# A batched matmul limited by its transfers: all loads first and all stores after, in place of loads mixed with stores

## The chip, the cores and the metric

The kernel runs on one core of a Trainium2 chip, the other cores idle. The metric is device time in microseconds (us), the median of several executions. A profile is one further execution; its span runs from the first to the last instruction and is about 2 us shorter than the device time.

Names: PE is the matmul engine (TensorE), ACT is ScalarE, DVE is VectorE, POOL is GpSimd, SP is the engine that issues the transfers here. In lines of the profile PEld is PE loading the stationary operand, and a q after an engine's name (SPq) is its sequencer, which issues instructions; PSUM is the memory that PE writes to. The granted clock is the share of PE's full clock that the trace records as let through. A transfer is cut over the core's 16 DMA engines, and the trace has a record of every packet: start, duration, size. A packet here is one contiguous run of one partition: 4 KB for loads, 16 KB for stores (8 KB for eight of them in the kernel before). Means of packet durations below are taken over all packets of a size in the trace. "Landings" are the semaphore updates of a transfer, one from each DMA engine.

## The reference

```python
batch, n_heads, seq_t, seq_s, channels = 8, 12, 512, 512, 64
x: (8, 12, 512, 64) float32        y: (8, 12, 512, 64) float32
out = np.einsum('bhtc,bhsc->bhts', x, y)     # (8, 12, 512, 512) float32
```

There are 96 heads. The inputs are 25.17 MB and the output 100.66 MB, so four fifths of all bytes are stores.

## The kernel before

Heads are taken in 12 groups of 8. A group's x and y are loaded as float32 (two loads of 1 MB), cast to bf16 by POOL, transposed by PE, copied out of PSUM by DVE and ACT, and then used in four results of two heads each (2 MB). Groups are pipelined: loads run three groups ahead, the transposes of group g + 1 are mixed into the results of group g, and each result is stored as soon as it is made.

```python
AHEAD = 3
lpool = tile_pool(bufs=AHEAD)      # loads, float32
bpool = tile_pool(bufs=2)          # bf16
tpool = tile_pool(bufs=2)          # transposed, bf16
opool = tile_pool(bufs=6)          # results, 16 KB per partition
...
def prepare(g, made):              # a generator, five steps
    ...                            # POOL casts x and y of group g to bf16
    if g + AHEAD < NG:
        load(g + AHEAD)
    yield
    ...                            # 16 transposes of y on PE, copies by DVE and ACT; then x
...
for g in range(NG):
    xT, yT = made.pop(g)
    steps = prepare(g + 1, made) if g + 1 < NG else iter(())
    for a in range(2):
        for pair in range(2):
            ot = opool.tile([P, K, S], fp32)
            edge = (g == 0 and a == 0) or (g == NG - 1 and a == 1)
            for k in range(K // 2):
                if (pair * K // 2 + k) in (0, 3, 6):
                    next(steps, None)
                pm = pmpool.tile([P, 2, S], fp32)
                ...                # 4 matmuls of 64x512 into pm
                ...                # ACT (k even) or DVE (k odd) copies pm to ot
                if edge and k % 2 == 1:
                    ...            # the first two and last two results: stored in halves of 1 MB
            if not edge:
                nc.sync.dma_start(ov[g, 2 * a + pair], otf)
```

Of the kernel before, what the change touches and what calls it, by code (L numbers as in the profile page):

```python
# [1 line left out]

# [5 lines left out]


@with_exitstack  # L10
def kernel(
    ctx: ExitStack,
    tc: tile.TileContext,
    x: bass.AP,
    y: bass.AP,
    out: bass.AP,
):





    nc = tc.nc
    B, H, T, C = x.shape
    _, _, S, _ = y.shape
    P = 128
    G = 4
    Q = P // G
    R = T // Q
    NG = B * H // (2 * G)  # L30
    K = R // 2
    AHEAD = 3
    fp32 = mybir.dt.float32
    bf16 = mybir.dt.bfloat16
    COPY = mybir.ActivationFunctionType.Copy
    assert C * 2 == P and S == T and R == 16

    xv = x.rearrange("b h t c -> (b h t c)").rearrange("(g a p n) -> g p a n", a=2, p=P, n=R * C)
    yv = y.rearrange("b h t c -> (b h t c)").rearrange("(g a p n) -> g p a n", a=2, p=P, n=R * C)
    ov = out.rearrange("b h t s -> (b h t s)").rearrange("(g a p n) -> g a p n", a=4, p=P, n=K * S)  # L40

    const = ctx.enter_context(tc.tile_pool(name="const", bufs=1))
    lpool = ctx.enter_context(tc.tile_pool(name="lpool", bufs=AHEAD))
    bpool = ctx.enter_context(tc.tile_pool(name="bpool", bufs=2))
    tpool = ctx.enter_context(tc.tile_pool(name="tpool", bufs=2))
    opool = ctx.enter_context(tc.tile_pool(name="opool", bufs=6))
    ptpool = ctx.enter_context(tc.tile_pool(name="ptpsum", bufs=2, space=bass.MemoryType.PSUM))
    pmpool = ctx.enter_context(tc.tile_pool(name="pmpsum", bufs=3, space=bass.MemoryType.PSUM))

    loaded = {}  # L50

    def load(g):
        xs = lpool.tile([P, 2, R, C], fp32)
        ys = lpool.tile([P, 2, R, C], fp32)
        nc.sync.dma_start(ys.rearrange("p a r c -> p a (r c)"), yv[g])  # L55
        nc.sync.dma_start(xs.rearrange("p a r c -> p a (r c)"), xv[g])  # L56
        loaded[g] = (xs, ys)

    for g in range(AHEAD):
        load(g)  # L60

    ident = const.tile([P, P], bf16)
    make_identity(nc, ident)

    def prepare(g, made):

        xs, ys = loaded.pop(g)
        yb = bpool.tile([P, R, 2, C], bf16)
        xb = bpool.tile([P, R, 2, C], bf16)
        for s, b in ((ys, yb), (xs, xb)):  # L70
            for half in range(2):
                rows = slice(half * K, (half + 1) * K)
                nc.gpsimd.tensor_copy(b[:, rows], s[:, :, rows].rearrange("p a r c -> p r a c"))  # L73
        if g + AHEAD < NG:
            load(g + AHEAD)
        yield
        yT = tpool.tile([P, G * Q, R], bf16)
        xT = tpool.tile([P, K, P, 2], bf16)
        for half in range(2):
            pt = ptpool.tile([P, K, P], bf16)  # L80
            for k in range(K):
                nc.tensor.transpose(  # L82
                    pt[:, k, :], yb[:, half * K + k].rearrange("p a c -> p (a c)"), ident
                )
            dst = yT[:, :, half * K:(half + 1) * K]
            src = pt.rearrange("p k n -> p n k")
            if half == 0:
                nc.vector.tensor_copy(dst, src)  # L88
            else:
                nc.scalar.activation(dst, src, COPY)  # L90
            yield
        for half in range(2):
            pt = ptpool.tile([P, K, P], bf16)
            for k in range(K):
                e, i = divmod(k, K // 2)
                nc.tensor.transpose(  # L96
                    pt[:, k, :], xb[:, e * K + half * K // 2 + i].rearrange("p a c -> p (a c)"), ident
                )
            dst = xT[:, half * K // 2:(half + 1) * K // 2]
            src = pt.rearrange("p (e i) n -> p i n e", e=2)  # L100
            if half == 0:
                nc.vector.tensor_copy(dst, src)  # L102
            else:
                nc.scalar.activation(dst, src, COPY)  # L104
            yield
        made[g] = (xT, yT.rearrange("p n k -> p (n k)"))

    made = {}
    for _ in prepare(0, made):
        pass  # L110
    for g in range(NG):
        xT, yT = made.pop(g)
        steps = prepare(g + 1, made) if g + 1 < NG else iter(())
        for a in range(2):
            for pair in range(2):
                ot = opool.tile([P, K, S], fp32)
                otf = ot.rearrange("p r s -> p (r s)")
                edge = (g == 0 and a == 0) or (g == NG - 1 and a == 1)
                for k in range(K // 2):
                    if (pair * K // 2 + k) in (0, 3, 6):  # L120
                        next(steps, None)
                    pm = pmpool.tile([P, 2, S], fp32)
                    for two in range(2):
                        for h in range(2):
                            col = (2 * pair + h) * Q
                            nc.tensor.matmul(  # L126
                                pm[h * 64:(h + 1) * 64, two, :],
                                xT[a * C:(a + 1) * C, 2 * k + two, col:col + Q].rearrange("c n e -> c (n e)"),
                                yT[a * C:(a + 1) * C, (2 * pair + h) * S:(2 * pair + h + 1) * S],
                                start=True, stop=True,  # L130
                            )
                    if k % 2 == 0:
                        nc.scalar.activation(ot[:, 2 * k:2 * k + 2, :], pm, COPY)  # L133
                    else:
                        nc.vector.tensor_copy(ot[:, 2 * k:2 * k + 2, :], pm)  # L135
                    if edge and k % 2 == 1:
                        i, j = (2 * k - 2) * S, (2 * k + 2) * S
                        nc.sync.dma_start(ov[g, 2 * a + pair][:, i:j], otf[:, i:j])
                if not edge:
                    nc.sync.dma_start(ov[g, 2 * a + pair], otf)  # L140


# [1 line left out]
_INS = ['x', 'y']  # L144
_OUTS = [((8, 12, 512, 512), 'float32')]


# [23 lines left out]
```

## Time and profile before

| | before |
|---|---|
| time, median (3 runs) | 306.62 us (306.41 to 306.93) |
| profiled span | 304.3 us |
| q1 (all loads and stores), share of 16 engines' time | 98.2% |
| PE, DVE, ACT busy | 69%, 48%, 39% |
| mean packet: 4 KB load, 8 KB store, 16 KB store | 163.4, 309.4, 612.3 ns |
| landings of the last store: first, mean, last | 296.6, 298.7, 303.2 us |

From the page of the kernel before: the span; then the span in 40 slices (PE busy and DMA busy in tenths, PE's granted clock in tenths, GB/s moved); then the queue of all loads and stores, and the queue of instruction fetches (count, MB, share of 16 engines).

```profile
span 304.3 us, 2968 instructions
PE   0899999999959538928946844893897797671000
PEclk9999999999999855555555655555555555555555
DMA  7999999999999999999999999999999999999992
GB/s 283 411 410 418 436 429 423 419 442 405 445 419 419 430 431 421 420 437 424 426 426 435 414 429 433 413 433 429 433 433 429 431 433 429 428 428 433 423 420 89
q1 hardware_dynamic: 14016, 125.83, 98.2%
q8 instruction: 9, 0.15, 0.2%
```

DMA stays at 9 from the second slice to the last but one. That is the bound (q1 98.2% of 16 engines' time); PE has gaps (69% busy). The traffic is 410 to 433 GB/s over the longer stretches; single slices between the second and the last but one show 405 to 445.

One caution on the clock row: the trace's first clock record is at 98.0 us here, and the 9s before it have no record behind them. Transposes start 107 ns apart there (median), as in stretches recorded at 0.50.

The table of stretches of the kernel before (start:end, length, busy time of PE, weight load, DVE, ACT, POOL, PE's clock, DMA share, GB/s), first two stages, then the end:

```profile
12.00:20.00 8.00, 7.61 (x42) 3.29 (x43) 4.68 (x5) 4.06 (x4) 6.31 (x7) 1.00 1.03 410
180.00:220.00 40.00, 25.53 (x141) 13.16 (x141) 18.28 (x16) 14.70 (x15) 6.07 (x6) 0.50 1.01 429
...
295.00:300.00 5.00, 0.00 (x0) 0.00 (x0) 0.00 (x0) 0.00 (x0) 0.00 (x0) 0.50 0.57 243
300.00:304.30 4.30, 0.00 (x0) 0.00 (x0) 0.00 (x0) 0.00 (x0) 0.00 (x0) 0.50 0.08 34
```

Loads alone run at 410 GB/s, mixed traffic and stores at 424 to 433 (stretches of 10 us and more). The last two lines show a fade: for six microseconds only some of the 16 DMA engines still work (DMA share 0.57, then 0.08). The 16 landings of the last store come one by one, from 296.6 to 303.2 us. The kernel ends with the slowest engine (the span ends at 304.3 us).

### The profile page before, as it was taken

How to read it: one execution, taken by the hardware profiler on the slowest of the kernel's cores; microseconds unless marked ns; L12 is line 12 of the kernel's file. 1: busy time of each engine (PE TensorE's matmuls, PEld its weight loads, DVE VectorE, ACT ScalarE, POOL GpSimd, SP SyncE). 2: the span in 40 equal slices, each digit the busy share in tenths (PEclk: the TensorE clock that was granted, in tenths of full speed). 3: DMA queues.
4: the chain of work that ended last, by engine and by line, in shares of the span. 5: the costliest groups of instructions: out<-in, count | busy, mean ns of one | idle time of the engine just before them, and what ended most of it. 6: DMA issues, size and time to landing. Idle time of an engine off the chain costs nothing.

```text
span 304.3 us, 2968 instructions
## 1 busy us (share of the span) xinstructions
PE 208.5 (69%) x1152; PEld 104.6 (34%) x1152; DVE 144.7 (48%) x120; ACT 119.4 (39%) x121; POOL 49.3 (16%) x54
## 2 busy tenths in 40 slices
PE   0899999999959538928946844893897797671000
PEld 0444344555425114513613522541453443330000
DVE  0456666567446435616525733743565664443000
ACT  1454645364445224624515512542364552522000
POOL 3773220400500310230050050031000000000000
PEclk9999999999999855555555655555555555555555
DMA  7999999999999999999999999999999999999992
GB/s 283 411 410 418 436 429 423 419 442 405 445 419 419 430 431 421 420 437 424 426 426 435 414 429 433 413 433 429 433 433 429 431 433 429 428 428 433 423 420 89
DMA packets 14031, 126.03 MB, mean 414 GB/s; under 512 B 1216, under 2 KB 1216, under 8 KB 7360
## 3 DMA queue, kind: packets, MB, share of 16 engines
q1 hardware_dynamic: 14016, 125.83, 98.2%
q8 instruction: 9, 0.15, 0.2%
q14 instruction: 6, 0.05, 0.0%
HBM read 25.17 MB, written 100.66 MB: 413 GB/s over the span
## 4 chain that ended last, share of the span: by engine, by line
DMA 60%; PE 23%; DVE 4%; ACT 2%; issue 1%; POOL 1%; SPq 0%; ACTq 0%
DMA out_dram<-ot 48%; PE pm L126 17%; DMA xs<-in_x_dram 12%; PE pt L82 3%; PE pt L96 3%; DVE ot L135 2%; ACT ot L133 2%; DVE xT L102 1%; POOL xb L73 1%; SPq L55 0%; ACTq L133 0%; SPq L140 0%; ACT xT L104 0%; SPq L56 0%
## 5 line engine op out<-in xcount | busy, mean ns | idle before, releaser
L126 PE MATMUL pm<-yT,xT 64*64 64x512 bf16 x768 | 164.0, 610 | 56.0 <-ACT ot L133 53.9
L135 DVE COPY ot<-pm 128x1024 f32<-128x1024 f32 x96 | 117.2, 1223 | 113.3 <-PE pm L126 57.3
L133 ACT ACTIVATE ot<-pm 128x1024 f32<-128x1024 f32 x96 | 95.1, 1023 | 113.7 <-DMA out_dram<-ot 81.2
L126 PEld LDWEIGHTS <-xT 64*64 64x64 bf16 x768 | 66.1, 150 | 131.2 <-issue 122.7
L73 POOL CAST yb<-ys 128x1024 bf16<-128x1024 f32 x24 | 24.3, 1040 | 140.5 <-DMA ys<-in_y_dram 94.7
L82 PE MATMUL pt<-ident,yb 128*128 128x128 bf16 x192 | 23.7, 307 | 10.7 <-POOL yb L73 6.9
L73 POOL CAST xb<-xs 128x1024 bf16<-128x1024 f32 x24 | 24.3, 1040 | 16.3 <-issue 6.9
L82 PEld LDWEIGHTS <-yb 128*128 128x128 bf16 x192 | 19.9, 143 | 20.3 <-issue 11.5
L96 PE MATMUL pt<-ident,xb 128*128 128x128 bf16 x192 | 24.9, 310 | 1.1 <-POOL xb L73 0.9
L96 PEld LDWEIGHTS <-xb 128*128 128x128 bf16 x192 | 19.1, 141 | 19.3 <-issue 17.8
L104 ACT ACTIVATE xT<-pt 128x1024 bf16<-128x1024 bf16 x12 | 12.3, 1024 | 32.9 <-PE pt L96 29.4
L102 DVE COPY xT<-pt 128x1024 bf16<-128x1024 bf16 x12 | 14.7, 1223 | 10.8 <-PE pt L96 9.4
L88 DVE COPY yT<-pt 128x1024 bf16<-128x1024 bf16 x12 | 14.6, 1216 | 8.9 <-PE pt L82 8.9
L90 ACT ACTIVATE yT<-pt 128x1024 bf16<-128x1024 bf16 x12 | 12.3, 1022 | 9.3 <-PE pt L82 7.7
L90 ACT ACT_TABLE_LOAD x1 | 1.3, 1283 | 0.7 <-PEq L155 0.7
masks.py:199 POOL TENSOR_SCALAR_AFFINE_SELECT ident<-ident 128x128 bf16<-128x128 bf16 x1 | 0.3, 292 | 0.1
masks.py:197 POOL MEMSET ident<- 128x128 bf16 x1 | 0.2, 204 | 0.3 <-POOLq L155 0.3
L155 POOL MEMSET const-float32-0.0<- 128x1 f32 x1 | 0.1, 98 | 0.2 <-issue 0.2
L155 POOL MEMSET const-bfloat16-1.0<- 128x1 bf16 x1 | 0.1, 101 | 0.0
L155 POOL MEMSET const-uint8-127<- 128x1 uint8 x1 | 0.1, 101 | 0.0
L155 POOL MEMSET const-float32-1.0<- 128x1 f32 x1 | 0.1, 98 | 0.0
## 6 DMA issues: line engine op xcount, KB each, us to landing
out_dram<-ot SPq DMA_DIRECT2D x44, 2048.0 KB, 28.3
ys<-in_y_dram SPq DMA_DIRECT2D x12, 1024.0 KB, 20.3
xs<-in_x_dram SPq DMA_DIRECT2D x12, 1024.0 KB, 22.2
out_dram<-ot SPq DMA_DIRECT2D x8, 1024.0 KB, 21.0
```

The source lines that it names most:

```text
L73: nc.gpsimd.tensor_copy(b[:, rows], s[:, :, rows].rearrange("p a r c -> p r a c"))
L82: nc.tensor.transpose(pt[:, k, :], yb[:, half * K + k].rearrange("p a c -> p (a c)"), ident)
L88: nc.vector.tensor_copy(dst, src)
L90: nc.scalar.activation(dst, src, COPY)
L96: nc.tensor.transpose(pt[:, k, :], xb[:, e * K + half * K // 2 + i].rearrange("p a c -> p (a c)"), ident)
L102: nc.vector.tensor_copy(dst, src)
L104: nc.scalar.activation(dst, src, COPY)
L126: nc.tensor.matmul(pm[h * 64:(h + 1) * 64, two, :], xT[a * C:(a + 1) * C, 2 * k + two, col:col + Q].rearrange("c n e -> c (n e)"), yT[a * ...
L133: nc.scalar.activation(ot[:, 2 * k:2 * k + 2, :], pm, COPY)
L135: nc.vector.tensor_copy(ot[:, 2 * k:2 * k + 2, :], pm)
L155: nc = _bacc.Bacc("TRN2", target_bir_lowering=False, num_devices=1)
```

## The change

The intent: never mix reads and writes of memory, by loading everything first. The transposed x and y of all groups stay on chip as bf16: 12 groups x 8 KB, 96 KB of each partition. The six 16 KB buffers that received loads then become the six buffers of the results. All 48 stores are whole tiles of 2 MB.

```diff
-    AHEAD = 3
+    NB = 6
-    lpool = ...(bufs=AHEAD)   bpool (bufs=2)   tpool (bufs=2)   opool (bufs=6)
+    dpool = ctx.enter_context(tc.tile_pool(name="dpool", bufs=NB))
+    bpool = ctx.enter_context(tc.tile_pool(name="bpool", bufs=3))
+    xpool = ctx.enter_context(tc.tile_pool(name="xpool", bufs=NG))
+    ypool = ctx.enter_context(tc.tile_pool(name="ypool", bufs=NG))
...
-                edge = (g == 0 and a == 0) or (g == NG - 1 and a == 1)
-                    if edge and k % 2 == 1:
-                        i, j = (2 * k - 2) * S, (2 * k + 2) * S
-                        nc.sync.dma_start(ov[g, 2 * a + pair][:, i:j], otf[:, i:j])
-                if not edge:
-                    nc.sync.dma_start(ov[g, 2 * a + pair], otf)
+    def result(o, steps):
+        ot = buffer()                       # from dpool, as the loads
+        for k in range(K // 2):
+            next(steps, None)
+            ...                             # matmuls and copies as before
+        nc.sync.dma_start(ov[o], ot)
+    for g in range(NB + 1):
+        for _ in prepare(g):
+            pass
+    for o in range(G * NG):
+        g = NB + 1 + o
+        result(o, prepare(g) if g < NG else iter(()))
```

More of the change, by code (lines that the diff above doesn't have):

```diff
@@ L35, with buffer @@
     COPY = mybir.ActivationFunctionType.Copy
-    assert C * 2 == P and S == T and R == 16
+    assert C * 2 == P and S == T and R == 16 and 4 * R * C == K * S
     xv = x.rearrange("b h t c -> (b h t c)").rearrange("(g a p n) -> g p a n", a=2, p=P, n=R * C)
     yv = y.rearrange("b h t c -> (b h t c)").rearrange("(g a p n) -> g p a n", a=2, p=P, n=R * C)
-    ov = out.rearrange("b h t s -> (b h t s)").rearrange("(g a p n) -> g a p n", a=4, p=P, n=K * S)
+    ov = out.rearrange("b h t s -> (b h t s)").rearrange("(o p n) -> o p n", p=P, n=K * S)
     const = ctx.enter_context(tc.tile_pool(name="const", bufs=1))
-    lpool = ctx.enter_context(tc.tile_pool(name="lpool", bufs=AHEAD))
-    bpool = ctx.enter_context(tc.tile_pool(name="bpool", bufs=2))
-    tpool = ctx.enter_context(tc.tile_pool(name="tpool", bufs=2))
-    opool = ctx.enter_context(tc.tile_pool(name="opool", bufs=6))
+    dpool = ctx.enter_context(tc.tile_pool(name="dpool", bufs=NB))
+    bpool = ctx.enter_context(tc.tile_pool(name="bpool", bufs=3))
+    xpool = ctx.enter_context(tc.tile_pool(name="xpool", bufs=NG))
+    ypool = ctx.enter_context(tc.tile_pool(name="ypool", bufs=NG))
     ptpool = ctx.enter_context(tc.tile_pool(name="ptpsum", bufs=2, space=bass.MemoryType.PSUM))
     pmpool = ctx.enter_context(tc.tile_pool(name="pmpsum", bufs=3, space=bass.MemoryType.PSUM))
+    def buffer():
+        data = dpool.tile([P, K * S], fp32)
+        return data
     loaded = {}
     def load(g):
-        xs = lpool.tile([P, 2, R, C], fp32)
-        ys = lpool.tile([P, 2, R, C], fp32)
-        nc.sync.dma_start(ys.rearrange("p a r c -> p a (r c)"), yv[g])
-        nc.sync.dma_start(xs.rearrange("p a r c -> p a (r c)"), xv[g])
-        loaded[g] = (xs, ys)
-    for g in range(AHEAD):
+        data = buffer()
+        n = 2 * R * C
+        for i, v in enumerate((yv, xv)):
+            nc.sync.dma_start(data[:, i * n:(i + 1) * n].rearrange("p (a n) -> p a n", a=2), v[g])
+        loaded[g] = [data[:, i * n:(i + 1) * n].rearrange("p (a r c) -> p a r c", a=2, r=R) for i in range(2)]
+    for g in range(NB):
         load(g)
@@ L63, with prepare @@
     make_identity(nc, ident)
-    def prepare(g, made):
-        xs, ys = loaded.pop(g)
-        yb = bpool.tile([P, R, 2, C], bf16)
-        xb = bpool.tile([P, R, 2, C], bf16)
-        for s, b in ((ys, yb), (xs, xb)):
+    made = {}
+    def prepare(g):
+        halves = []
+        for s in loaded.pop(g):
+            b = bpool.tile([P, R, 2, C], bf16)
             for half in range(2):
@@ L73, in prepare @@
                 nc.gpsimd.tensor_copy(b[:, rows], s[:, :, rows].rearrange("p a r c -> p r a c"))
-        if g + AHEAD < NG:
-            load(g + AHEAD)
-        yield
-        yT = tpool.tile([P, G * Q, R], bf16)
-        xT = tpool.tile([P, K, P, 2], bf16)
+            halves.append(b)
+        yb, xb = halves
+        if g + NB < NG:
+            load(g + NB)
+        yT = ypool.tile([P, G * Q, R], bf16)
+        xT = xpool.tile([P, K, P, 2], bf16)
         for half in range(2):
@@ L106, in prepare @@
         made[g] = (xT, yT.rearrange("p n k -> p (n k)"))
-    made = {}
-    for _ in prepare(0, made):
-        pass
-    for g in range(NG):
-        xT, yT = made.pop(g)
-        steps = prepare(g + 1, made) if g + 1 < NG else iter(())
-        for a in range(2):
-            for pair in range(2):
-                ot = opool.tile([P, K, S], fp32)
-                otf = ot.rearrange("p r s -> p (r s)")
-                edge = (g == 0 and a == 0) or (g == NG - 1 and a == 1)
-                for k in range(K // 2):
-                    if (pair * K // 2 + k) in (0, 3, 6):
-                        next(steps, None)
-                    pm = pmpool.tile([P, 2, S], fp32)
-                    for two in range(2):
-                        for h in range(2):
-                            col = (2 * pair + h) * Q
-                            nc.tensor.matmul(
-                                pm[h * 64:(h + 1) * 64, two, :],
-                                xT[a * C:(a + 1) * C, 2 * k + two, col:col + Q].rearrange("c n e -> c (n e)"),
-                                yT[a * C:(a + 1) * C, (2 * pair + h) * S:(2 * pair + h + 1) * S],
-                                start=True, stop=True,
-                            )
-                    if k % 2 == 0:
-                        nc.scalar.activation(ot[:, 2 * k:2 * k + 2, :], pm, COPY)
-                    else:
-                        nc.vector.tensor_copy(ot[:, 2 * k:2 * k + 2, :], pm)
-                    if edge and k % 2 == 1:
-                        i, j = (2 * k - 2) * S, (2 * k + 2) * S
-                        nc.sync.dma_start(ov[g, 2 * a + pair][:, i:j], otf[:, i:j])
-                if not edge:
-                    nc.sync.dma_start(ov[g, 2 * a + pair], otf)
@@ new lines, in result @@
+    def result(o, steps):
+        g, rest = divmod(o, G)
+        a, pair = divmod(rest, 2)
+        xT, yT = made[g]
+        ot = buffer()
+        otv = ot.rearrange("p (r s) -> p r s", s=S)
+        for k in range(K // 2):
+            next(steps, None)
+            pm = pmpool.tile([P, 2, S], fp32)
+            for two in range(2):
+                for h in range(2):
+                    col = (2 * pair + h) * Q
+                    nc.tensor.matmul(
+                        pm[h * 64:(h + 1) * 64, two, :],
+                        xT[a * C:(a + 1) * C, 2 * k + two, col:col + Q].rearrange("c n e -> c (n e)"),
+                        yT[a * C:(a + 1) * C, (2 * pair + h) * S:(2 * pair + h + 1) * S],
+                        start=True, stop=True,
+                    )
+            if k % 2 == 0:
+                nc.scalar.activation(otv[:, 2 * k:2 * k + 2, :], pm, COPY)
+            else:
+                nc.vector.tensor_copy(otv[:, 2 * k:2 * k + 2, :], pm)
+        nc.sync.dma_start(ov[o], ot)
+        for _ in steps:
+            pass
@@ L144 @@
+    for g in range(NB + 1):
+        for _ in prepare(g):
+            pass
+    for o in range(G * NG):
+        g = NB + 1 + o
+        result(o, prepare(g) if g < NG else iter(()))
 _INS = ['x', 'y']
```

## The prediction

> **What bounds the kernel now.** The DMA engines. The page's queue table gives q1 98.2% of 16 engines' span; its slices show DMA at 9 tenths from the second to the 39th. The table of stretches gives 410 GB/s for 12 to 20 us (loads alone), 425 to 428 from 60 to 180 us (mixed) and 426 to 433 from 220 to 290 us (stores alone). [...] No compute engine is near a limit: PE 69% busy, DVE 48%, ACT 39%; in the waits view ACT and DVE wait 81 and 55 us for stores to land. At the end, traffic fades from 426 GB/s at 296 us to nothing at 303 us: one or two of the 16 engines finish about 6 us after the first. The landings of one DMA lie 0.3 us apart before 25 us, over 6 us at the end.
>
> **What the change removes, adds and moves.** Bytes stay: 25.17 MB read, 100.66 MB written. In the packet records a 4 KB load packet takes 163 ns, a 16 KB store packet 612 ns, an 8 KB one 309 ns.
> - Eight 1 MB stores become four of 2 MB. Per engine 64 x 309 ns becomes 32 x 612 ns: -0.2 us.
> - Loads and stores no longer mix. A load packet takes 159 to 161 ns mixed with stores, 163.5 ns in the pure load stage after 9 us. Of 384 per engine about 270 move from mixed to pure: estimate +0.5 to +1 us, less what packets overlap. Stores take 612 to 613 ns either way.
> - Per engine, after: 384 x 163.3 ns + 384 x 612.4 ns = 298 us; the same sum for before is 298 us.
> - The instruction stream is as long as before, so its fetches (q8, q14) still hold a few engines back: I keep the 6 us fade.
> - PE, ACT, DVE and POOL do the same instructions in another order; all off the path.
>
> **Is there a bubble between the phases?** The one step that could cost. Loads go on 5.2 us per group and end near 65 us. The seventh group lands near 40 us and is transposed by 44 us. The first five results each carry one group's transposes: PE spends about 3.6 us on a result and 3.5 us on 32 transposes (timeline, 30 to 60 us), so 7 to 8 us each. The stores are ready near 51, 58, 66, 73 and 80 us; DMA wants them at 65, 70, 75, 80 and 85 us. Afterwards a result costs PE 3.4 to 4.4 us against 4.9 us of DMA, and six buffers give 29 us of queue, as now. So no bubble, with 5 us of slack at its narrowest.
>
> **Predicted time.** 306.6 us, 8 in 10 between 304.5 and 309.5. Chances: faster by over 2%: 0.03; within 2%: 0.92; slower by over 2%: 0.05.
>
> **What would show each step.** GB/s near 410 up to about 65 us, then 428 to 431 flat, no dip between 60 and 95 us; DMA 9 tenths throughout; load packets near 163 ns, store packets near 612 ns; the fade again 5 to 7 us; PE clock low in the load phase; waits of ACT and DVE for landings only in the store phase.
>
> **What would make it wrong.** Transposes at half clock, or late casts, making the first five results slower than about 9 us each: a dip after 65 us, each us paid in full. Pure loads slower than 410 GB/s when twelve are queued. Or the load phase, where engines stay in step, absorbing some of the fade: 1 to 3 us faster.

What the prediction says of the hardware has these figures in the trace of the kernel before. Fetches: the nine on q8 took 888 to 1108 ns each, and the 16 landings of one load lay 0.5 us apart up to the first of them (at 23.3 us; the prediction has 0.3) and 1.8 us apart in the next load. In step: the same 0.5 us. Half clock, or low clock: a recorded 0.50, with transposes 107 ns apart, and 107 ns (median) in the first 20 us too, where no clock is recorded.

## The result and the profile after

The changed kernel took 308.32 us (median of 4, 307.69 to 308.73) against 306.77 us for the kernel before. The ratio is 1.0049, with a 95% interval of 1.0026 to 1.0073. Ratios here are the mean time of one kernel's runs over that of the other's of the same rounds, so they are not quite the ratio of the medians. The change costs half a per cent: within 2%, and inside the predicted range, but not for the predicted reasons. The profiled execution of the changed kernel is the slowest of its four (308.73 us), so traces overstate the difference by about 1 us.

| | before | after |
|---|---|---|
| profiled span | 304.3 us | 307.0 us |
| mean 4 KB load packet | 163.4 ns | 164.7 ns |
| mean 16 KB store packet | 612.3 ns | 617.3 ns |
| mean time a DMA engine idles between 60 and 110 us | 0.05 us | 2.74 us |
| landings of the last store: first, mean, last | 296.6, 298.7, 303.2 us | 302.9, 303.6, 306.1 us |

The same lines of the page, for the changed kernel:

```profile
span 307.0 us, 2985 instructions
PE   1887766789899858677676757675776757671000
PEclk9999986599555555555555555555555555555555
DMA  7999999969999999999999999999999999999994
GB/s 281 413 410 409 409 410 407 409 274 436 414 433 416 427 425 429 425 429 427 421 431 426 429 423 427 427 429 423 431 425 425 429 423 431 423 425 429 431 425 205
q1 hardware_dynamic: 13440, 125.83, 98.1%
```

The two phases are plain: 409 GB/s for eight slices, then a hole of 274, then 414 to 436. The stretches around the hole and at the end:

```profile
60.00:64.00 4.00, 2.83 (x36) 2.26 (x35) 2.77 (x3) 2.67 (x4) 2.92 (x4) 0.86 0.99 391
64.00:66.00 2.00, 1.93 (x23) 1.20 (x21) 2.00 (x3) 2.00 (x3) 1.57 (x3) 1.00 0.09 35
66.00:68.00 2.00, 2.00 (x19) 0.91 (x18) 1.99 (x2) 1.31 (x3) 1.90 (x2) 1.00 0.61 262
...
295.00:300.00 5.00, 0.00 (x0) 0.00 (x0) 0.00 (x0) 0.00 (x0) 0.00 (x0) 0.50 0.99 423
300.00:304.30 4.30, 0.00 (x0) 0.00 (x0) 0.00 (x0) 0.00 (x0) 0.00 (x0) 0.50 0.69 293
```

From 64 to 66 us the DMA engines do almost nothing (share 0.09): the loads are all but done and no store has been issued. In the packet records fewer than four engines work from 64.30 to 66.78 us. The end fades more steeply than before: the engines now finish within 3.2 us of each other, not 6.6.

Why was no store there? The timeline of the changed kernel has what came before the first store (start, duration, engine, line, operation; in brackets the idle time before it and what ended that):

```profile
57.21 1.87 PE L91 MATMUL pt<-ident,b 128*128 128x128 bf16 x16 [1.11 <-ACT xT L113]
59.54 1.89 PE L105 MATMUL pt<-ident,b 128*128 128x128 bf16 x16 [0.46 <-DVE yT L97]
...
61.47 1.02 ACT L113 ACTIVATE xT<-pt 128x1024 bf16<-128x1024 bf16 x1 [1.33 <-PE pt L105]
62.38 1.94 ACT L137 ACTIVATE data<-pm 128x1024 f32<-128x1024 f32 x2
...
65.92 0.36 SPq L140 DMA_DIRECT2D out_dram<-data  x1
```

The first copy of a result (line 137) starts at 62.38 us, directly after the transposes of the tenth group (lines 91 to 113), and not after those of the seventh. The instruction order on ACT, as built, shows that this is no accident of timing (my build listing, which is not kept with the runs; the ACT instructions of the trace stand in the same order, ten copies of yT and ten of xT before the first of `data`):

```
18 Activation yT<-pt 128x128x8
19 Activation xT<-pt 128x1024
20 Activation yT<-pt 128x128x8
21 Activation xT<-pt 128x1024          (the 20th of such copies: the tenth group)
22 Activation data<-pm 128x1024 x2     (the first result)
```

The scheduler of the language, which decides the order at build time, had put ten groups ahead of the first result. This could be read before the prediction was made; I had looked at that listing and not counted.

So the traces name three differences: a gap of 2.4 us, store packets that take 5 ns longer (0.8%), and a smaller spread of the engines at the end. The experiments have to say which of them cost what, whether the pure phases themselves are at fault, and what makes the packets slow.

### The profile page after: what moved, and what is told of

Its sections match the earlier page's. It is cut to its first block, busy times and chain, and to the rows that moved or that the text cites. A ratio compares the mean times of both kernels' runs of the same rounds, so it can differ in the third digit from the quotient of the medians.

```text
span 307.0 us, 2985 instructions
## 1 busy us (share of the span) xinstructions
PE 200.0 (65%) x1152; PEld 108.1 (35%) x1152; DVE 145.9 (48%) x120; ACT 119.2 (39%) x121; POOL 49.3 (16%) x54
## 4 chain that ended last, share of the span: by engine, by line
DMA 63%; PE 16%; ACT 6%; DVE 3%; SPq 1%; POOL 1%; issue 1%; ACTq 0%; POOLq 0%; DVEq 0%
DMA out_dram<-data 51%; PE pm L130 11%; DMA data<-in_x_dram 6%; DMA data<-in_y_dram 6%; ACT data L137 4%; DVE data L139 3%; PE pt L91 2%; PE pt L105 2%; SPq L63 1%; ACT xT L113 1%; ACT yT L99 1%; POOL b L81 1%; ACTq L137 0%; SPq L140 0%; POOLq L81 0%
## 5 line engine op out<-in xcount | busy, mean ns | idle before, releaser
L130 PE MATMUL pm<-yT,xT 64*64 64x512 bf16 x768 | 159.3, 601 | 56.6 <-ACT data L137 52.1
L139 DVE COPY data<-pm 128x1024 f32<-128x1024 f32 x96 | 117.3, 1224 | 96.6 <-DMA out_dram<-data 56.1
L137 ACT ACTIVATE data<-pm 128x1024 f32<-128x1024 f32 x96 | 94.1, 1022 | 119.0 <-DMA out_dram<-data 107.7
L130 PEld LDWEIGHTS <-xT 64*64 64x64 bf16 x768 | 73.0, 148 | 137.7 <-issue 128.6
L81 POOL CAST b<-data 128x1024 bf16<-128x1024 f32 x48 | 48.6, 1040 | 18.0 <-DMA data<-in_y_dram 10.0
L91 PE MATMUL pt<-ident,b 128*128 128x128 bf16 x192 | 19.7, 279 | 16.8 <-POOL b L81 7.9
L105 PE MATMUL pt<-ident,b 128*128 128x128 bf16 x192 | 22.2, 289 | 5.8 <-DVE yT L97 2.8
L91 PEld LDWEIGHTS <-b 128*128 128x128 bf16 x192 | 17.4, 128 | 20.1 <-issue 12.0
L105 PEld LDWEIGHTS <-b 128*128 128x128 bf16 x192 | 18.4, 134 | 12.3 <-issue 10.4
```

The lines of the kernel that those rows point to most:

```text
L81: nc.gpsimd.tensor_copy(b[:, rows], s[:, :, rows].rearrange("p a r c -> p r a c"))
L91: nc.tensor.transpose(pt[:, k, :], yb[:, half * K + k].rearrange("p a c -> p (a c)"), ident)
L105: nc.tensor.transpose(pt[:, k, :], xb[:, e * K + half * K // 2 + i].rearrange("p a c -> p (a c)"), ident)
L130: nc.tensor.matmul(pm[h * 64:(h + 1) * 64, two, :], xT[a * C:(a + 1) * C, 2 * k + two, col:col + Q].rearrange("c n e -> c (n e)"), yT[a * ...
L137: nc.scalar.activation(otv[:, 2 * k:2 * k + 2, :], pm, COPY)
L139: nc.vector.tensor_copy(otv[:, 2 * k:2 * k + 2, :], pm)
```

## The experiments

Each ran beside the kernel before on the same chip. The rounds ran on different chips (medians of the kernel before 306.38 to 306.56 us), so rows are best compared by their ratios. This table collects what their traces and times show. "Idle" is the mean time of a DMA engine without a packet between 60 and 110 us.

| kernel | idle, us | load, ns | store, ns | last store lands: first, last | time, us | ratio to before |
|---|---|---|---|---|---|---|
| after | 2.74 | 164.7 | 617.3 | 302.9, 306.1 | 308.32 | 1.0049 |
| a_program_order | 1.91 | 164.9 | 617.1 | 302.0, 304.8 | 307.75 | 1.0036 |
| a_all_prepared | 11.19 | 164.9 | 617.3 | 311.4, 314.4 | 316.97 | 1.0340 |
| dma_phases (wrong) | 0.03 | 164.8 | 611.5 | 297.6, 298.4 | 301.09 | 0.9822 |
| dma_mixed (wrong) | 0.03 | 163.8 | 611.1 | 297.1, 298.4 | 300.96 | 0.9818 |
| b_results_first | 1.53 | 165.1 | 617.0 | 301.6, 304.3 | 306.88 | 1.0018 |
| dma_gap (wrong) | 2.94 | 164.9 | 616.9 | 302.8, 303.1 | 306.23 | 0.9994 |
| before_aligned | 0.04 | 162.1 | 612.3 | 296.5, 301.9 | 304.81 | 0.9950 |
| before_split_n | 0.01 | 162.9 | 613.2 | 296.9, 305.9 | 308.76 | 1.0078 |
| c_no_gap | 0.02 | 164.5 | 612.8 | 297.7, 303.5 | 305.95 | 0.9981 |
| c_no_gap_aligned | 0.02 | 161.2 | 612.5 | 296.1, 301.8 | 304.43 | 0.9931 |
| dma_gap_stagger (wrong) | 3.28 | 164.8 | 616.0 | 303.4, 304.4 | 306.89 | 1.0008 |

### a_program_order

```diff
+    keep = tc.keep_in_program_order
-                nc.tensor.transpose(...)          # and every matmul, activation, tensor_copy
+                keep(nc.tensor.transpose(...))
```

> The changed kernel with every PE, ACT and DVE instruction pinned to the order of the program, so the first result follows the seventh group's transposes and not the tenth's. Theory A (the gap between the phases is paid in full): the first store is issued near 51 us, before the last load lands near 64 us; the dip at 64 to 67 us goes; the time falls by about 2.4 us against the changed kernel, to 305.5 to 306.3 us, ratio to the kernel before 0.996 to 0.999. Theory B (the gap was partly given back, because it let the 16 DMA engines line up again): the dip goes, but the landings of the last store spread 4 to 6 us instead of 3, and the time falls by 0.5 to 1.5 us, ratio 1.000 to 1.004. Theory C (the pure phases themselves are slow): the dip goes and the time stays, ratio 1.004 to 1.006.

The first store was issued at 53.3 us, as expected, and the hole at 64 us was gone. But a new hole opened later, which none of the three theories had allowed for:

```profile
78.00:80.00 2.00, 2.00 (x16) 0.99 (x14) 0.47 (x1) 1.50 (x2) 0.00 (x0) 0.50 0.96 410
80.00:82.00 2.00, 2.00 (x15) 0.99 (x14) 1.89 (x2) 0.56 (x1) 0.00 (x0) 0.50 1.01 434
82.00:84.00 2.00, 2.00 (x12) 0.80 (x11) 0.60 (x1) 1.43 (x2) 0.00 (x0) 0.50 0.65 270
84.00:86.00 2.00, 2.00 (x12) 1.04 (x11) 1.46 (x2) 1.07 (x2) 0.00 (x0) 0.50 0.37 156
```

PE is busy all the time here, at a recorded clock of 0.50: a result with a group's transposes takes it 7.8 us (stores were issued at 53.3, 61.2, 69.0, 76.8 and 84.7 us), while the DMA engines use up a store every 4.9 us (8 packets of 612 ns on each). From 60 to 120 us the profile shows PE busy for 60.00 us and the recorded clock stays at 0.50; what kept it there was not looked into. The prediction had named this risk, but only for results slower than 9 us. The run moved the gap rather than removing it, so it does not decide between the theories: its time is above what A expected, its spread at the end (2.8 us) below what B expected. It does hold a hint: store packets took 612.4 ns before the hole (66 to 82 us) and 617.6 ns after it (90 to 290 us).

### a_all_prepared

```diff
-    for g in range(NB + 1):
+    for g in range(NG):                  # on top of a_program_order
-        g = NB + 1 + o
+        g = NG + o
```

> The same pinned order, but all twelve groups are transposed before the first result: the gap is made larger on purpose. The last group is transposed near 70 us and the first store issued near 74 us, so the DMA engines idle for about 9 us after the loads, 6.5 us more than in the changed kernel. Theory A: time 6 to 7 us over the changed kernel, near 315 us, ratio to before 1.025 to 1.030. Theory B: the same 6 to 7 us over the changed kernel (the engines are already lined up by its gap), but 8 to 9 over a_program_order minus 1 to 2 us. Theory C says nothing of this run. If the idle time were hidden, the time would stay near 308 us.

The first store was issued at 74.4 us, and the DMA engines idled 11.19 us, 8.45 more than in the changed kernel. The time rose by 8.65 us (316.97 against 308.32). Against a_program_order, of the same rounds and with the same pinned order, 9.28 us more of idle time cost 9.22 us. Once there is a gap, each further microsecond of it is paid in full. Store packets stayed at 617.3 ns: a long gap does no more to them than a short one.

### dma_phases and dma_mixed

These two have transfers alone: the loads as in the kernels, and 48 stores of four constant tiles. One has two phases, the other the order of the kernel before.

```diff
     for g in range(NG):                  # dma_phases
         load(g)
     for o in range(G * NG):
         store(o)                         # ots[o % 4], written once by a memset
---
-    for g in range(NG):                  # dma_mixed
+    for g in range(5):
         load(g)
     for o in range(G * NG):
         store(o)
+        if o % G == 1 and 5 + o // G < NG:
+            load(5 + o // G)
```

> Transfers alone, results wrong on purpose: the 24 loads, then 48 stores of four constant tiles, with no TensorE, ScalarE or GpSimd work and a short instruction stream. Theory C: load packets near 163 ns and store packets near 617 ns, as in the changed kernel, since they come of the pure phases; time 300 to 303 us. Theory D (the slower packets come of the engines' compute traffic): 159 and 611 ns, time 297 to 299 us. If the end's spread comes of instruction fetches, the 16 landings of the last store lie within 1 us of each other here.

> Transfers alone again, results wrong on purpose, loads spread between the stores as in the kernel before (five groups first, then one group after each four stores). Theory C: 1.5 to 2.5 us faster than dma_phases, with load packets near 160 ns and store packets near 612 ns. Otherwise: within 0.5 us of dma_phases. If mixing is what spreads the engines, the last landings lie 3 us or more apart here and within 1 us in dma_phases; if instruction fetches do, within 1 us in both.

The GB/s of the 40 slices, dma_phases first, dma_mixed second:

```profile
GB/s 279 414 408 411 410 409 409 410 423 447 427 423 442 431 423 431 442 423 420 453 423 420 447 427 423 445 429 423 438 436 423 420 453 423 420 453 420 423 426 311
```

```profile
GB/s 279 412 410 433 429 421 421 440 416 439 423 416 441 434 413 430 431 434 412 436 427 412 438 440 411 437 425 445 427 421 442 434 421 434 442 421 429 445 422 285
```

The times are 301.09 and 300.96 us. Mixing reads and writes costs nothing here, so there was nothing for the change to win: its intent is refuted by this pair. Both are about 5.5 us faster than the kernel before, with every byte moved; that is what all the rest of the kernel (computing, its instruction fetches, its waits) costs the transfers. Neither theory fits both packets. In the two-phase one the load packets are as slow as in the real kernel (164.8 ns, as C has it), but the store packets are fast (as D has it): 611 ns flat up to 265 us. So pure phases alone do not make stores slow. After 265 us they rose, to 612 to 617 ns in stretches of 10 us, without a gap; I come back to this exception.

The last landings lie within 0.8 and 1.3 us, against 6.6 us with a full instruction stream. Mixing does not spread the engines.

### before_split_n

```diff
+                            for part in range(2):
+                                N = S // 2
-                                yT[..., (2 * pair + h) * S:(2 * pair + h + 1) * S],
+                                yT[..., at:at + N],     # two matmuls of 256 columns for one of 512
```

> The kernel before with each 512-column matmul cut into two of 256, so that PE's instruction stream grows from 2304 to 3840 instructions and its fetches from 9 to about 15; same data, same transfers. Theory G (the end's spread over the DMA engines comes of instruction fetches): the last landings spread 9 to 11 us instead of 6.6 and the time grows by 2 to 4 us, to 308.5 to 310.5 us. If it does not come of them: spread 6 to 7 us and 306 to 307 us, as PE has 30% of the span to spare.

The queue table of this kernel, instruction fetches in the last two lines:

```profile
q1 hardware_dynamic: 14016, 125.83, 97.4%
q8 instruction: 15, 0.25, 0.3%
q14 instruction: 6, 0.05, 0.0%
```

The fetches on q8 went from 9 to 15, the last landings from 6.6 to 9.0 us apart, and the time from 306.38 to 308.76 us, while the first engine finished as before (296.9 us). Theory G's numbers are met, at the lower end: six fetches more went with 2.4 us more of spread and of time. In the trace of the kernel before a fetch on q8 took 0.9 to 1.1 us, and a store packet that began as a fetch ended was slow: behind the fetch of 922 ns at 231.9 us it took 1018 ns in place of 611, and behind three others 975 to 1018. That the nine fetches of the kernel before make up the whole of its 6.6 us is not shown: the dma kernels, with no fetch on q8, lack the computing as well.

### b_results_first

```diff
+    convert(NB + 1)                      # POOL casts, split off from prepare
+    result(0, iter(()))
+    for o in range(1, G * NG):           # two results first, then one group after each result
+        result(o, iter(()))
+        g = NB + o
+        if g < NG:
+            for _ in prepare(g): pass
+            if g + 1 < NG: convert(g + 1)
```

> Two phases with no gap anywhere: the pinned order, but the first two results are computed before the eighth group is transposed, and each later group after a result and not within it. Ready times estimated from a_program_order's pace (4 us a result, 4 us a group): 48, 52, 60, 68, 75, 83, 91 us against 64, 69, 74, 79, 84, 89, 94 us wanted. Theory E (a gap puts the 16 engines into a state in which store packets take 616 to 618 ns to the end; without one they take 611 to 613 ns): no slice under 405 GB/s between 30 and 295 us, store packets at most 613 ns in the mean, time 305.0 to 306.5 us, ratio to the kernel before 0.995 to 1.000. Rival F (the slower store packets come of two phases with compute beside them, gap or not): store packets 616 to 618 ns, time 306.5 to 307.5 us, ratio 1.000 to 1.003.

The premise failed again. A result and a group took 8.3 us one after the other, not 8, and the seventh store was issued at 94.1 us, too late:

```profile
90.00:92.00 2.00, 2.00 (x12) 0.91 (x10) 0.80 (x1) 1.35 (x2) 0.00 (x0) 0.50 0.99 418
92.00:94.00 2.00, 2.00 (x12) 0.93 (x9) 1.57 (x2) 1.27 (x2) 0.00 (x0) 0.50 0.53 221
94.00:96.00 2.00, 2.00 (x14) 0.86 (x12) 1.30 (x2) 1.37 (x2) 0.00 (x0) 0.50 0.67 287
```

Still, it weighs against rival F: store packets took 612.4 ns from 68 to 88 us, with two phases and computing, and 617.6 ns from 98 to 290 us, after the gap. The switch moved with the gap, from 66 us (after) to 84 us (a_program_order) to 94 us.

### dma_gap

```diff
+    nc.vector.tensor_copy(ots[0][:, :2 * R * C], last[0])   # last[0]: the last loaded tile
     for o in range(G * NG):
         store(o)                                            # on top of dma_phases
```

> dma_phases with one gap made on purpose (results wrong on purpose): the first store's tile is written by a DVE copy out of the last loaded tile, so all DMA engines run dry for about 3 to 4 us after the loads. Theory E: store packets go from 611 ns to 615 to 618 ns for the rest of the run, and the time rises by the gap plus 1.5 to 2.5 us, to 305.5 to 307 us. Rival F: packets stay at 611 to 612 ns and the time rises by the gap alone, to 304 to 305 us.

```profile
62.00:64.00 2.00, 0.00 (x0) 0.00 (x0) 1.00 0.91 360
64.00:66.00 2.00, 1.23 (x1) 0.00 (x0) 1.00 0.00 0
66.00:68.00 2.00, 0.00 (x0) 0.00 (x0) 1.00 0.76 319
```

(Columns: DVE, POOL, clock, DMA share, GB/s.) The gap was 2.8 us, with 2.94 us idle. The time rose by 5.14 us: the gap, and 384 store packets per engine x 5.4 ns = 2.1 us. Packets took 616.9 ns on average, and 616 to 617 in nearly every stretch from 75 to 265 us, with no computing at all. Theory E holds, in its purest form.

The packet records show the two states more sharply than the means. From 100 to 260 us, 94 to 100% of the store packets took exactly 611 ns in the seven kernels without a gap, and 19 to 38% in the six with one; the rest were mostly 2 to 20 ns longer.

### c_no_gap

```diff
-    NB = 6                               # on top of b_results_first
+    NB = 4
+    rpool = ctx.enter_context(tc.tile_pool(name="rpool", bufs=2))      # for results only
+    bpool bufs=5; xpool, ypool bufs=NG - 1
-        ot = buffer()
+        ot = rpool.tile([P, K * S], fp32, name="early") if o % 6 < 2 else buffer()
+    for g in range(7):
+        convert(g); prepare(g)
+        if g in (1, 3):
+            result(g // 2, none)         # stored behind the last load
...
+    for o in range(2, G * NG):
+        result(o, prepare(o + 5) if o + 5 < NG else none)
```

> Two phases again, made so that no store can come late: two of the six buffers serve results only, so the first two results are computed inside the load phase (after the second and the fourth group), their stores are queued behind the last load, and five groups are still to transpose while stores run. Ready times estimated from the pace of 7.8 us for a result with a group: 54, 62, 70, 77, 85, 88 us for stores 2 to 7, wanted at 72, 77, 82, 87, 92, 96 us. Theory E (a gap switches the store packets from 611-612 ns to 616-618 ns for the rest of the run): no slice under 405 GB/s from 10 to 295 us, store packets 611 to 613 ns throughout, time 305.5 to 306.5 us, ratio to the kernel before 0.996 to 1.001. If store packets are 616 to 618 ns after 95 us though no gap is there, theory E is not the whole cause, and the time is 306.5 to 307.5 us.

```profile
64.00:66.00 2.00, 2.00 (x16) 0.95 (x12) 1.32 (x2) 0.71 (x1) 1.79 (x2) 0.50 1.00 412
66.00:68.00 2.00, 2.00 (x16) 0.95 (x12) 1.04 (x1) 1.31 (x2) 0.31 (x1) 0.50 0.96 410
68.00:70.00 2.00, 2.00 (x16) 0.95 (x12) 1.35 (x2) 0.63 (x1) 1.72 (x2) 0.50 1.02 434
```

The page's slices:

```profile
GB/s 274 413 407 409 412 404 411 410 432 428 431 435 424 431 424 435 426 433 428 433 425 433 426 435 424 435 424 437 424 435 424 441 420 439 418 441 416 444 416 103
```

No gap (0.02 us idle), store packets 612.8 ns in the mean and 612.7 from 90 to 290 us, 305.95 us. Theory E's expectation is met, but for one slice of the load phase at 404 GB/s where it allowed 405. Against the changed kernel this is 0.7% or about 2 us (1.0049 to 0.9981), with the same two phases. The spread at the end is back too: 297.7 to 303.5 us. So the smaller spread of the changed kernel goes with the gap, not with the load phase.

### before_aligned and c_no_gap_aligned

```diff
+    pad = const.tile([P, 32], fp32)      # 128 bytes per partition
+    nc.vector.memset(pad, 0.0)
     ident = const.tile([P, P], bf16)
```

> The kernel before with 128 bytes of padding, so that its load and store tiles start at a multiple of 256 bytes in each partition instead of 128 above one. [...] If not: 611 and 159 ns, and 306 to 307 us.

> The same with 128 bytes of padding, so that the buffers start at a multiple of 256 bytes in each partition, as in before_aligned, where load packets took 159 ns in the pure load stage instead of 163.5 ns and the time fell by 1.6 us. Here all 384 load packets of an engine lie in the pure load stage: 384 x 4.5 ns is 1.7 us. Expected: load packets 159 to 160 ns, loads done by about 63 us instead of 65, time 303.8 to 305.0 us, ratio to the kernel before 0.990 to 0.996.

"If not" is the case in which the padding does nothing. Only these two start addresses were run.

In the tile addresses of the built programs (a listing that is not kept with the runs), load and result buffers begin at 128 modulo 256; the pad makes that 0. In the pure load stage (9 to 22 us) load packets fell from 163.4 to 159.0 ns. Store packets did not move (612.3 ns). before_aligned takes 304.81 us (0.9950, interval 0.9935 to 0.9965): better than the 306 to 307 us expected if the padding does nothing. The load packets explain only part of the 1.6 us: 384 x 1.3 ns (162.1 for 163.4 in the mean) is 0.5 us, and the mean landing of the last store came 0.6 us earlier (298.1 for 298.7). The rest is a smaller spread at the end, 5.4 us in place of 6.6, whose cause was not looked into.

In c_no_gap_aligned all loads lie in that stage. Its stretches show 420 GB/s for loads where the unaligned kernels have 409, and 430 for stores:

```profile
20.00:60.00 40.00, 27.28 (x256) 19.73 (x255) 22.05 (x19) 18.45 (x19) 31.26 (x32) 0.80 1.03 420
100.00:140.00 40.00, 33.94 (x164) 17.20 (x163) 24.50 (x20) 20.61 (x21) 0.00 (x0) 0.50 1.01 430
```

It takes 304.43 us, ratio 0.9931 (0.9919 to 0.9944), and beats both kernels, as expected. It does not clearly beat before_aligned, which keeps the old structure and adds two lines.

### dma_gap_stagger

```diff
+    keep(nc.sync.dma_start(ov[G * NG - 1][:8, :K * S // 2], ots[0][:8, :K * S // 2]))
     for o in range(G * NG):              # on top of dma_gap
         store(o)
```

> dma_gap with one more small store ahead of the 48 (8 partitions of 8 KB, into a place that the last store overwrites; results wrong on purpose). It falls on some of the 16 DMA engines and not on the others, and shifts those by about 0.3 us when all start again after the gap. Theory H (the slow state comes of how the engines stand to each other when they start together): the mean store packet changes clearly from 616.9 ns, towards 611 to 613 ns, and the time falls by 1 to 2 us from dma_gap's 306.2 us. Rival I (having run dry is enough, however they start): 616 to 618 ns again and 306 to 307 us.

Store packets took 616.0 ns in the mean (614.6 from 80 to 100 us, 616.5 after 180 us), and 306.89 us. That is what rival I expected. The shift was larger than planned: the eight packets of the small store took 1.0 to 1.7 us each. A shift of some engines at the restart, at least of this size, does not restore the fast state. What the state is stays open.

## Why the prediction was right or wrong

The time was right (306.6 predicted, 308.32 measured, range 304.5 to 309.5), and so was the core of it: the DMA engines bound both kernels, and the same bytes take the same time in either order. dma_mixed and dma_phases, 0.13 us apart, show this best. That the error stayed small is partly luck: two steps failed at a cost of 4.4 us in the profiled run, and a third was off by 2.0 us the other way. Step by step:

- **"So no bubble, with 5 us of slack at its narrowest."** This step failed. The idle measured 2.74 us per engine. "The seventh group lands near 40 us and is transposed by 44 us", and the stores "ready near 51" took the program's text for the engines' order. As built, the tenth group came first and the first store was issued at 65.9 us. Even in the text's order the step fails, at another place (82 to 86 us in a_program_order): a result with a group took 7.8 us where the list of ready times used 7.3, the first of them was ready at 53 and not at 51, and a store's first packet starts 0.8 us after its issue (84.7 and 85.5 us). The engines also wanted it sooner than the list's 85 us: they had idled 1.9 us in the mean by 85.5. a_all_prepared shows that each such microsecond is paid in full.
- **"Stores take 612 to 613 ns either way."** Wrong: 617.3 ns, 384 x 5 ns = 1.9 us per engine. Theory E gives the reason as far as runs can: in all six kernels with a gap store packets took 616.0 to 617.3 ns in the mean, in the others 611.1 to 613.2, and the switch came with the gap wherever it lay.
- **"I keep the 6 us fade."** Mis-sized: 3.2 us. That fetches add to it fits before_split_n (six more fetches, 2.4 us more). But the last engine landed 2.5 us after the mean one, against 4.5 before, and this gave 2.0 us back. All four computing kernels with a gap spread by 2.7 to 3.2 us, the five without one (c_no_gap among them) by 5.4 to 9.0, so it came with the gap. How is not shown. Three of the changed kernel's nine fetches (24.2, 45.9 and 63.9 us) fall before the gap. Theory B would have an engine that is behind catch up in it, and this is near the prediction's own last risk ("absorbing some of the fade: 1 to 3 us faster"). Or the slower packets hide the fast engines' lead. No run separates the two.
- **"A load packet takes ... 163.5 ns in the pure load stage", estimate +0.5 to +1 us.** Measured 163.3 ns from 9 to 22 us, and 164.7 over all loads against 163.4: 384 x 1.3 ns = +0.5 us. Right, though the mixed load packets of the kernel before took 162.2 ns in the mean (after 30 us) and not "159 to 161 ns". The cause of the 163.5 was not asked; before_aligned shows that 128 bytes of start address take it to 159.0.
- **"-0.2 us" for whole tiles.** Not tested by itself. It is a difference of packet durations that the trace of before shows, and it is too small to see in these times.

The sum for the profiled runs: idle 2.7, stores 384 x 617.3 less the 235.3 us of before's stores = 1.7, loads 0.5, together +4.9 us for the mean engine (298.7 to 303.6). The last engine gains 2.0 of it back, so +2.9 us from 303.2 to 306.1. Medians show +1.5 us: the profiles caught the slowest execution of the changed kernel and a fast one of the kernel before (306.08 us).

Theory E was formed only after a_program_order had hinted at it, and has one exception that the runs do not explain: dma_phases, without a gap, went to 612 to 617 ns by itself after 265 us. So a gap is sufficient in these runs, but not the only way in. Why the packets stay slow is not shown. dma_gap rules out the computing, and a_all_prepared the length of the gap; the one test of how the engines restart did not support that either.

## What to carry to other kernels

When transfers bound a kernel, ask first what the transfers take alone, in the old and the new order: two kernels without any compute settled here, within 0.13 us, that the idea had nothing to win. When a change creates a phase boundary, count in the built instruction order which work stands ahead of the first store, and budget the slowest engine until the last mixed result, not only at the boundary. Keep the DMA queue from running dry even once: here it cost the gap and about 2 us more. And try the start addresses of the tiles: here 128 bytes of padding gave 0.5%.
